# A two-image convolution: three loads move one pair later in the queue, nine fp32 buffers and five bf16 ones in place of eight and six

## The chip, the core and the metric

The kernel runs on one core of a Trainium2 chip. The metric is device microseconds of one execution. Engines are named as in the profile: PE (TensorE, matrix products), DVE (VectorE), ACT (ScalarE), POOL (GpSimd), SP (SyncE, which here only issues transfers). The core has 16 DMA engines, which move data between HBM and on-chip memory.

## The reference

A 3 x 3 convolution with padding 1 over 16 images of 64 channels and 64 x 64 points, to 128 output channels, all in fp32. About 90% of the weights are zero, but the kernel treats them as dense.

```python
x_pad = np.pad(x, ((0, 0), (0, 0), (pad, pad), (pad, pad)), mode='constant')
for b, co, ci, kh, kw in ...:          # all of them, written as nested loops
    output[b, co] += weight[co, ci, kh, kw] * x_pad[b, ci, kh:kh+h, kw:kw+w]
```

Input is 16.8 MB, output 33.6 MB.

## The kernel before, in words

**Pairs.** Two images make a pair: their 64 channels each fill the 128 partitions. There are eight pairs, 0 to 7. `load(p)` brings pair p (2 MB, 16 KiB a partition) into an fp32 buffer of the pool `f`; the queue is SP's. `cast_x` turns it into a bf16 buffer of the pool `x`, in pieces of rows that ACT, POOL and (for pair 0) DVE take. The two results of a pair, one of 2 MB for each image, are written into two more buffers of the same pool `f` and stored from there. So the pool `f` serves loads and results alike, in the order in which the program asks for them: a new one takes a buffer that an older load or result has left, and its first writer waits until the casts have read the old load, or the store of the old result has landed.

**Blocks.** A pair is worked in four blocks of 16 rows. In a block of `twos` (all but the first block of pair 0), POOL adds neighbouring rows into `s` (L161), PE multiplies `s` by the middle row of taps, ACT copies that shared product from PSUM to `pc` (L168), and PE makes two further products, for the even and the odd rows; DVE adds each to `pc` and writes the result buffer (L175). A block is 30 matmuls on PE, one addition on POOL, two copies on ACT and four additions on DVE. `s` has three buffers, so POOL works up to three blocks ahead of PE. [...] `direct` does the same for one block with nine taps a row.

**Casts.** A hand-written table says after which block of which pair a piece is cast. For the inputs 4 to 7 it is filled by a loop: in pair p, after block 1, ACT casts rows 0 to 16 of input p + 2; after block 3 ACT casts rows 16 to 32 and POOL rows 32 to 64.

**The order.** Each engine executes its instructions in the order in which the program writes them (the schedule is manual). SP's queue holds the weights, loads 0 to 4, and then for each pair its two stores and one further load; the last pair is stored in four halves. A transfer that has to wait holds up those behind it on SP. The loop is this:

```python
for p in range(NP):
    o = [f_pool.tile([C_OUT, H, W], FP32, name="f") for _ in range(2)]
    ...                                 # the four blocks and their casts
    if not last:
        for n in range(2):
            nc.sync.dma_start(out=out[2 * p + n], in_=o[n])
    if p + 5 < NP:
        load(p + 5)
```

Below, L5 is load 5, 3A and 3B are the results of pair 3 or their stores, and x4 is the bf16 buffer of pair 4.

Of the kernel before, what the change touches and what calls it, by code (L numbers as in the profile page):

```python
# [27 lines left out]
def kernel(  # L28
# [11 lines left out]
    NP = B // 2  # L40
    HEAD = 32

    const_pool = ctx.enter_context(tc.tile_pool(name="const", bufs=1))
    x_pool = ctx.enter_context(tc.tile_pool(name="x", bufs=6))
    s_pool = ctx.enter_context(tc.tile_pool(name="s", bufs=3))
    p_pool = ctx.enter_context(tc.tile_pool(name="pc", bufs=4))

    f_pool = ctx.enter_context(tc.tile_pool(name="f", bufs=8))
    psum_pool = ctx.enter_context(
        tc.tile_pool(name="psum", bufs=8, space=bass.MemoryType.PSUM)  # L50
    )
# [7 lines left out]
    def load(p, *cuts):  # L59
        src = x[2 * p : 2 * p + 2].rearrange("n i h w -> (n i) h w")  # L60
        raw[p] = f_pool.tile([128, H, W], FP32, name="f")
        for a, b in zip((0, *cuts), (*cuts, H)):
            nc.sync.dma_start(out=raw[p][:, a:b, :], in_=src[:, a:b, :])

    def cast_x(copy, p, a, b):
        if p not in xs:
            xs[p] = x_pool.tile([128, H, W], BF16, name="x")
        copy(out=xs[p][:, a:b, :], in_=raw[p][:, a:b, :])  # L68
# [82 lines left out]
    def direct(p, o, r0, rows):  # L151
        ps = product(
            [(xs[p], G1, r0, 1), (xs[p], G0, r0 - 1, 1), (xs[p], G2, r0 + 1, 1)], rows
        )
        nc.scalar.copy(out=o[0][:, r0 : r0 + rows, :], in_=ps[0])  # L155
        nc.vector.tensor_copy(out=o[1][:, r0 : r0 + rows, :], in_=ps[1])  # L156

    def twos(p, o, r0):
        t0 = r0 // 2
        s = s_pool.tile([128, 8, W], BF16, name="s")  # L160
        nc.gpsimd.tensor_tensor(  # L161
            out=s, in0=xs[p][:, r0 : r0 + 16 : 2, :], in1=xs[p][:, r0 + 1 : r0 + 16 : 2, :], op=ADD
        )
        shared = product([(s, G1, 0, 1)], 8)
        pc = []
        for n in range(2):
            c = p_pool.tile([128, 8, W], FP32, name="pc")
            nc.scalar.copy(out=c, in_=shared[n])  # L168
            pc.append(c)
        even = [(xs[p], G21, r0 + 1, 2), (xs[p], G0, r0 - 1, 2)]  # L170
        odd = [(xs[p], G01, r0, 2), (xs[p], G2, r0 + 2, 2)]
        for first, terms in ((r0, even), (r0 + 1, odd)):
            ps = product(terms, 8)
            for n in range(2):
                nc.vector.tensor_tensor(  # L175
                    out=o[n][:, first : r0 + 16 : 2, :], in0=ps[n], in1=pc[n], op=ADD
                )


    ACT, POOL = nc.scalar.copy, nc.gpsimd.tensor_copy  # L180
    casts = {
        (0, 1): [(POOL, 0, 48, H)],
        (0, 2): [(ACT, 1, 0, 16)],
        (0, 3): [(ACT, 1, 16, 32), (POOL, 1, 32, H)],
        (1, 0): [(ACT, 2, 0, 16)],
        (1, 1): [(ACT, 2, 16, 32), (POOL, 2, 32, H)],
        (1, 2): [(ACT, 3, 0, 16)],
        (1, 3): [(ACT, 3, 16, 32), (POOL, 3, 32, H)],
    }
    for p in range(2, 6):  # L190
        casts[p, 1] = [(ACT, p + 2, 0, 16)]
        casts[p, 3] = [(ACT, p + 2, 16, 32), (POOL, p + 2, 32, H)]

    for p in range(NP):
        o = [f_pool.tile([C_OUT, H, W], FP32, name="f") for _ in range(2)]
        last = p == NP - 1
        for blk in range(4):
            r0 = 16 * blk
            if BLOCKS[p][blk] == "T":
                twos(p, o, r0)  # L200
            else:
                for r, rows in ((r0, 8), (r0 + 8, 8)):
                    direct(p, o, r, rows)
            for cast_of in casts.get((p, blk), ()):
                cast_x(*cast_of)
            if last and blk % 2 == 1:
                for n in range(2):
                    rows = slice(r0 - 16, r0 + 16)
                    nc.sync.dma_start(out=out[2 * p + n][:, rows, :], in_=o[n][:, rows, :])
        if not last:  # L210
            for n in range(2):
                nc.sync.dma_start(out=out[2 * p + n], in_=o[n])
        if p + 5 < NP:
            load(p + 5)


# [28 lines left out]
```

## Time and profile before

| | us |
|---|---|
| median of 5 runs | 128.56 (128.5 to 128.68) |
| the profiled execution | 128.62 |
| its span in the profile | 126.8 |
| PE busy | 109.9 (87%) |
| DVE busy | 82.4 (65%) |
| ACT busy | 52.3 (41%) |
| POOL busy | 50.6 (40%) |
| data queue, share of 16 DMA engines | 95.5% |

The span runs from the first to the last instruction that the profiler saw; the time of an execution has 1.8 us around it. The profile gives busy time for each engine, the span in 40 slices of 3.17 us, and for each idle stretch of an engine the event that ended it (the releaser). A transfer has an issue on SP's timeline and a time to landing; it has landed when all DMA engines that share it are done.

### The profile page before, as it was taken

The page shows a single profiled execution, that of the slowest core. Times are in us where ns is not written, and L with a number is a line of the kernel's source. Part 1 is how long each engine was busy: PE and PEld are TensorE (multiplying, and loading weights), DVE is VectorE, ACT ScalarE, POOL GpSimd, SP SyncE. Part 2 cuts the span into 40 slices and gives each one's busy share as a digit, 9 for nine tenths or more (in the row PEclk, how much of TensorE's full clock was granted, in tenths as well). Part 3 has the DMA queues.
Part 4 walks back from the last instruction along what each step waited for, and adds up shares of the span by engine and source line. Part 5 has one row for each costly group of instructions (what it writes and reads, how often), then busy time and mean ns, then how long its engine had stood idle before and what let it go on. Part 6 is the DMA issues. An engine that isn't in the chain of part 4 may idle for free.

```text
span 126.8 us, 2519 instructions
## 1 busy us (share of the span) xinstructions
PE 109.9 (87%) x1002; PEld 61.0 (48%) x1002; DVE 82.4 (65%) x136; ACT 52.3 (41%) x85; POOL 50.6 (40%) x45
## 2 busy tenths in 40 slices
PE   6589999999999799969999999999999999992000
PEld 6334545567776255534555555555555555550000
DVE  0382577877760999239978778777877777776000
ACT  4542466666636336333636363636333333330000
POOL 2059613998375323913366335733333330000000
PEclk9968999999999999999999999999999999999855
DMA  4999999999999999999999999999999969999990
GB/s 134 413 444 429 434 429 429 419 264 429 439 419 424 429 426 444 419 421 429 434 429 419 434 419 434 429 419 431 424 434 434 413 284 413 419 411 413 424 393 36
DMA packets 4044, 50.79 MB, mean 400 GB/s; under 512 B 448, under 2 KB 448, under 8 KB 576
## 3 DMA queue, kind: packets, MB, share of 16 engines
q1 hardware_dynamic: 4032, 50.63, 95.5%
q8 instruction: 8, 0.13, 0.4%
q14 instruction: 4, 0.03, 0.1%
HBM read 17.07 MB, written 33.55 MB: 399 GB/s over the span
## 4 chain that ended last, share of the span: by engine, by line
PE 65%; DMA 19%; DVE 4%; issue 1%; DVEq 1%; SPq 0%
PE ps L142 65%; DMA out_dram<-f 15%; DMA f<-in_x_dram 4%; DVE f L175 4%; DVEq L240 0%; DVE x L68 0%; SPq L71 0%; DVEq L175 0%
## 5 line engine op out<-in xcount | busy, mean ns | idle before, releaser
L142 PE MATMUL ps<-x,wT 64*128 64x504 bf16 (+3 forms) x780 | 94.9, 378 | 2.2 <-DVE x L68 1.7
L175 DVE TENSOR_TENSOR f<-ps,pc 128x512 f32<-128x512 f32 x124 | 77.1, 685 | 25.9 <-PE ps L142 19.1
L142 PEld LDWEIGHTS <-wT 64*128 64x128 bf16 x966 | 57.8, 95 | 51.9 <-issue 7.5
L161 POOL TENSOR_TENSOR s<-x 128x512 bf16<-128x512 bf16 x31 | 35.6, 1155 | 52.0 <-PE ps L142 40.3
L168 ACT COPY pc<-ps 128x512 f32<-128x512 f32 x62 | 33.4, 589 | 53.7 <-issue 39.7
L142 PE MATMUL ps<-s,wT 64*128 64x512 bf16 (+1 forms) x186 | 30.1, 377 | 1.6 <-DVE f L175 1.6
L68 ACT CAST x<-f 128x1024 bf16<-128x1024 f32 (+2 forms) x16 | 16.3, 1026 | 0.7 <-DMA f<-in_x_dram 0.7
L68 POOL CAST x<-f 128x2048 bf16<-128x2048 f32 (+1 forms) x8 | 14.8, 1845 | 1.0 <-DMA f<-in_x_dram 1.0
L83 PE MATMUL ps<-idle_rhs 128*128 128x128 bf16 x27 | 2.9, 306 | 1.0 <-DVE idle_rhs L80 1.0
L83 PEld LDWEIGHTS <-idle_rhs 128*128 128x128 bf16 x27 | 2.8, 148 | 1.0 <-DVE idle_rhs L80 1.0
L97 DVE CAST w_bf<-w_sb 128x192 bf16<-128x192 f32 (+1 forms) x4 | 1.1, 351 | 2.7 <-DMA w_sb<-in_weight_dram 2.7
L155 ACT COPY f<-ps 128x512 f32<-128x512 f32 x2 | 1.2, 586 | 4.1 <-PE ps L142 4.1
L156 DVE COPY f<-ps 128x512 f32<-128x512 f32 x2 | 1.4, 692 | 2.2 <-PE ps L142 2.2
L68 DVE CAST x<-f 128x576 bf16<-128x576 f32 (+1 forms) x2 | 1.3, 641 | 2.1 <-DMA f<-in_x_dram 2.1
L97 ACT ACT_TABLE_LOAD x1 | 1.3, 1283 | 0.7 <-PEq L229 0.7
L97 ACT CAST w_bf<-w_sb 128x64 bf16<-128x64 f32 (+1 forms) x2 | 0.7, 418 | 1.6 <-DMA w_sb<-in_weight_dram 1.6
L103 PE MATMUL ps<-ident,w_bf 128*128 128x128 bf16 x9 | 0.9, 223 | 0.3 <-DVE w_bf L97 0.3
L107 DVE TENSOR_TENSOR wT<-ps,wT 128x384 bf16<-128x384 f32 x2 | 1.0, 548 | 0.0
L103 PEld LDWEIGHTS <-w_bf 128*128 128x128 bf16 x9 | 0.5, 98 | 0.7 <-DVE w_bf L97 0.7
L80 DVE MEMSET idle_rhs<- 128x64 uint32 x1 | 0.1, 112 | 0.8 <-PEq L229 0.8
L116 ACT CAST wT<-ps 128x384 bf16<-128x384 f32 x1 | 0.5, 479 | 0.2 <-PE ps L103 0.2
L118 DVE CAST wT<-ps 128x384 bf16<-128x384 f32 x1 | 0.6, 551 | 0.0
(7 smaller groups left out, 1.4 us busy)
## 6 DMA issues: line engine op xcount, KB each, us to landing
out_dram<-f SPq DMA_DIRECT2D x14, 2048.0 KB, 15.8
f<-in_x_dram SPq DMA_DIRECT2D x7, 2048.0 KB, 22.1
out_dram<-f SPq DMA_DIRECT2D x4, 1024.0 KB, 9.4
f<-in_x_dram SPq DMA_DIRECT2D x2, 1024.0 KB, 6.1
w_sb<-in_weight_dram SPq DMA_DIRECT2D x1, 288.0 KB, 2.9
```

What stands on the lines that cost most here:

```text
L68: copy(out=xs[p][:, a:b, :], in_=raw[p][:, a:b, :])
L83: nc.tensor.matmul(idle_ps, idle_rhs, idle_rhs, start=True, stop=True)
L97: copy(out=w_bf4[:, g, a:b, :], in_=w_v[:, k : k + b - a, :])
L103: nc.tensor.matmul(wps[:, j, :], src, ident, start=True, stop=True)
L107: nc.vector.tensor_tensor(out=wT[:, g], in0=wps, in1=wT[:, G1], op=SUB)
L118: nc.vector.tensor_copy(out=wT[:, G0], in_=ps0)
L142: nc.tensor.matmul(ps[n][:, lo:hi, c_lo:c_hi], tap(g, kw, n), src[q, a:b:step, c_lo + kw - 1 : c_hi + kw - 1], start=(i == 0), stop=(i == ...
L155: nc.scalar.copy(out=o[0][:, r0 : r0 + rows, :], in_=ps[0])
L156: nc.vector.tensor_copy(out=o[1][:, r0 : r0 + rows, :], in_=ps[1])
L161: nc.gpsimd.tensor_tensor(out=s, in0=xs[p][:, r0 : r0 + 16 : 2, :], in1=xs[p][:, r0 + 1 : r0 + 16 : 2, :], op=ADD)
L168: nc.scalar.copy(out=c, in_=shared[n])
L175: nc.vector.tensor_tensor(out=o[n][:, first : r0 + 16 : 2, :], in0=ps[n], in1=pc[n], op=ADD)
```

## The change

Three edits. The pool `x` has five buffers in place of six, the pool `f` nine in place of eight. The loads 5, 6 and 7 stand behind the stores of the pairs 1, 2 and 3 in SP's queue, where they stood behind those of the pairs 0, 1 and 2. ACT's first piece of the casts of inputs 4 to 7 stands after block 2 of its pair in place of block 1.

```diff
-    x_pool = ctx.enter_context(tc.tile_pool(name="x", bufs=6))
+    x_pool = ctx.enter_context(tc.tile_pool(name="x", bufs=5))
...
-    f_pool = ctx.enter_context(tc.tile_pool(name="f", bufs=8))
+    f_pool = ctx.enter_context(tc.tile_pool(name="f", bufs=9))
...
     for p in range(2, 6):
-        casts[p, 1] = [(ACT, p + 2, 0, 16)]
+        casts[p, 2] = [(ACT, p + 2, 0, 16)]
         casts[p, 3] = [(ACT, p + 2, 16, 32), (POOL, p + 2, 32, H)]
...
-        if p + 5 < NP:
-            load(p + 5)
+        if 5 <= p + 4 < NP:
+            load(p + 4)
```

## The prediction, made before the changed kernel was run

> **What bounds the kernel now.** I read the slices of the page first, for which resource is full all along; then the DMA queues; then stretches of the tail; last the timelines of the engines around the holes.
>
> The slices and the queue rows of the page (each digit is a fortieth of the span in tenths; a queue row gives packets, MB and share of 16 engines' span):
> ```profile
> PE   6589999999999799969999999999999999992000
> DMA  4999999999999999999999999999999969999990
> q1 hardware_dynamic: 4032, 50.63, 95.5%
> q8 instruction: 8, 0.13, 0.4%
> ```
> Both rows are full nearly throughout, but PE stops at slice 37 and DMA doesn't. 50.63 MB at the 427 to 430 GB/s of the middle stretches take 118 us of a span of 126.8: the transfers are the bound, and PE is close behind. PE has two holes, near slices 13 and 17; DMA has one, slice 32.
>
> The stretches around slice 32 and the end (us, PE clock, DMA share of 16 engines, GB/s):
> ```profile
> 98.00:101.00 3.00, 1.00 1.02 437
> ...
> 102.00:103.00 1.00, 1.00 0.39 164
> 103.00:104.00 1.00, 1.00 0.70 295
> 104.00:107.00 3.00, 1.00 1.01 426
> ...
> 122.00:124.00 2.00, 0.50 0.78 324
> 124.00:126.00 2.00, 0.50 0.10 41
> ```
> At 102 most DMA engines have run dry. They start again about 1.2 us after the next stores are issued at 102.84. But not all ran dry: store 5B (pair 5, second image) was issued at 90.64 and took 15.0 us to land whole, so some engine worked on it until 105.6. The last row says the same of the end: a share of 0.10 is 1.6 engines of 16. **The end is set by one or two late DMA engines that had no hole.** From 105.6 they land 6A at 110.7, 6B at 115.9, and the last store at 116.25 + 9.5 = 125.75. That is 20.15 us for 8.4 MB, where four spacings of the steady stretch (4.87 us for 2 MB) make 19.5. At most 0.65 us is to be had there.
>
> The holes of PE, in the DVE timeline (start, us, instruction, idle before and its releaser):
> ```profile
> 37.00 0.69 DVE L175 TENSOR_TENSOR f<-ps,pc 128x512 f32<-128x512 f32 x1 [0.69 <-POOL s L161]
> 41.37 7.27 DVE L175 TENSOR_TENSOR f<-ps,pc 128x512 f32<-128x512 f32 x12 [3.68 <-PE ps L142]
> ...
> 55.97 9.06 DVE L175 TENSOR_TENSOR f<-ps,pc 128x512 f32<-128x512 f32 x15 [4.16 <-DMA out_dram<-f]
> ```
> DVE waits twice for an output buffer whose store is under way: until 41.37 for that of store 0B (23.52 + 17.7 = 41.2; the label names PE, which was long done), until 55.97 for that of 1B (36.33 + 19.5 = 55.8). PSUM fills and PE waits in turn. Pairs start on PE (first product of s) at 34.77, 48.87, 63.46, 76.27, 89.07, 101.88 for pairs 2 to 7: pair 2 takes 14.1, pair 3 14.6, the rest 12.8. The stalls cost PE 3.1 us.
>
> [...] The trace agrees (0.39 of the engines busy at 102, whole landing at 105.6); so below every landing is that of the last engine. [...] The q8 row, 0.13 MB in 8 packets, fits that; I suppose, without a row for each engine, that these packets make some engines late. The change leaves PE's instructions as they are, so I keep the lateness.
>
> **The change part by part.** No instruction is added or removed. PE, DVE and POOL keep their order, SP moves three loads behind two stores each, ACT moves four casts by one block.
>
> *Stalls removed.* As built, the first writes of pair 2 wait for load 1's buffer and store 0A (landed 36.4, written from 37.7), those of pair 3 for 0B (41.2, against about 50) and a cast buffer. Both stalls go: pair 3 starts at 34.77 + 12.81 = 47.6, pair 4 at 60.4. The gain is 3.1 us of PE.
>
> *Loads later.* The queue is first in, first out and full, so places in it are times. From the issue and landing of each transfer before, the places after load 4 (31.5) land whole at 36.4, 41.2, 46.0, 51.0, 55.8, 61.3, 66.3, 71.1, 75.9, 80.9, 85.7. Before they are 0A 0B L5 1A 1B L6 2A 2B L7 3A 3B; after, 0A 0B 1A 1B L5 2A 2B L6 3A 3B L7. SP has issued each before its place comes (1A at 35.7; 2A by about 48.8; 3A by 61.6), so no gap opens. Behind a moved load on SP stand only the next pair's stores, which wait for DVE longer still; each takes SP 0.3 to 1.2 us to issue. L5 lands at 55.8, L6 at 71.1, L7 at 85.7, each 9.8 later, while pairs come sooner.
>
> *Who waits for a load.* POOL casts half of it, and its timeline in pair 4 shows how early:
> ```profile
> 64.61 1.16 POOL L161 TENSOR_TENSOR s<-x 128x512 bf16<-128x512 bf16 x1 [2.00 <-PE ps L142]
> 65.71 1.89 POOL L68 CAST x<-f 128x2048 bf16<-128x2048 f32 x1
> 67.80 1.15 POOL L161 TENSOR_TENSOR s<-x 128x512 bf16<-128x512 bf16 x1 [0.20 <-PE ps L142]
> ```
> The cast stands 2.25 us after the pair's start; behind it is the sum s for the next pair's first block, which PE needs 12.8 after the start. From landing to that product: 1.89 cast, 1.15 sum, 0.2 of hand-overs, 3.25 us. A landing later than 9.55 us after the pair's start stalls PE one for one. ACT's limit is nearly the same: the copy of the last block stands at +10.5 (73.99 in pair 4) and the cast ahead of it takes 1.06, so landing after +9.45 delays it and DVE behind it, by at most the PE stall itself; DVE has 0.6 to 0.7 us of idle time a block to catch up. I count no more for ACT.
> Pair 3: L5 at +8.2, no stall, POOL idles instead. Pair 4: L6 at 71.1 - 60.4 = +10.7, stall 1.15; pair 5 starts at 74.35. Pair 6 can start at 85.7 + 3.25 = 88.95 (stall 1.8). Before it was 89.07. **The 3.1 us are given back as waits for loads**, and the sum at pair 6 is -0.1.
>
> *The tail.* Pair 7 starts 0.1 earlier, 6A is issued at about 102.7, the early engines run dry as before, the late ones don't notice. Gain 0 to 0.3; I take 0.1. In pair 2 ACT's cast of x4 moves too: its load landed at 31.5 and its first reader, POOL, comes at about 52, so it costs nothing. Five bf16 buffers cost nothing: pair 5's takes that of pair 0, last read around 22. Both pools take 9 x 16 + 5 x 8 = 184 KiB a partition in place of 176.
>
> Sum: profiled 128.62 (span 126.8 and 1.8 around it) less 0.1; the median of the runs is 0.06 lower, and with half of the possible 0.3 in place of 0.1 I say **128.4**.
>
> **The rivals.**
> *Loads come in time (faster).* The share falls from 101 on; less the 1.2 us of start, 6A issued by about 100, nearly 3 us sooner than worked out, leaves no engine dry, and if what the late engines lose after 102 comes of all starting together, they save up to the 0.65: about 127.95. That needs L7 by 83. For it: the places carry 2 to 3 us of lateness of single engines, which may differ. Against: the loads' places follow from bytes alone.
> *Waits for loads overtake the slack (slower).* The late engines are free at 105.6; less 1.2 us of start, 6A may be issued up to 104.4, 1.6 later than before. That is L7 landing later than 87.4. From there each microsecond adds one: at 88.3, 129.4. It needs 2 to 3% less transfer rate before 86. For it: four stores now follow each other at 31 to 51, and PE twice waits on a load with nothing buffered. Against: stretches with loads mixed in (427 to 429) and of stores alone (427) have one rate.
> *The change doesn't do what it says.* The order as built shows the moved loads and the new waits, so I give this nothing.
> *The gain goes through whole (faster).* The 3.1 us show up in the end: 125.5. The full queue speaks against it; under 1 in 20.
>
> **How the numbers follow.** A measurement here tells about 0.2% (0.26 us) from no change. Stalls exchanged, tail as it was: 0.60, giving 128.1 to 128.85, mostly within the bound (0.48 same, 0.09 faster, 0.03 slower). Loads in time or gain whole: 0.23 (0.21 faster, 0.02 same). Slack overtaken: 0.17, all slower. Sum: faster 0.30, same 0.50, slower 0.20. The range 127.9 to 129.2 reaches into both outer cases; the likeliest case alone is 128.1 to 128.85.
>
> **What would show it.** DVE's two waits for stores gone, pair 3 at 47.6 and pair 4 at 60.4; POOL casts waiting for f loads at about 49.8 to 55.8, 62.6 to 71.1 and 76.6 to 85.7; PE stalled for s before pairs 5 and 6; pair 6 within half a microsecond of 89; slice 32 of DMA still low; the last landing near 125.6. Pair 6 before 88 or after 90.6, or a DMA row without a hole, would prove the working wrong.

## The result, and the profile after

Medians: 128.54 us for the changed kernel (43 runs), 128.65 for the kernel before (80 runs). The ratio is 0.9992, 95% interval 0.9981 to 1.0004: no difference that the measurement can tell. The prediction was 128.4 with "same" the likeliest. The profiled execution of the changed kernel took 129.26 us, so it stands 0.7 above its median and its span of 127.5 is compared with care.

The slices and the data queue in the page of the changed kernel:
```profile
PE   6689999999999999999999989996899999991000
DMA  4999999999999999999999999999999989999990
q1 hardware_dynamic: 4032, 50.63, 95.9%
```
PE's holes near slices 13 and 17 are gone. Two others have come, near slices 23 and 27. The DMA row is full as before, and its one weak slice is still slice 32.

DVE's timeline in pairs 2 and 3 of the changed kernel (start, us, instruction, idle before and its releaser):
```profile
38.26 2.48 DVE L175 TENSOR_TENSOR f<-ps,pc 128x512 f32<-128x512 f32 x4 [0.69 <-POOL s L161]
41.41 2.51 DVE L175 TENSOR_TENSOR f<-ps,pc 128x512 f32<-128x512 f32 x4 [0.67 <-PE ps L142]
...
50.96 2.53 DVE L175 TENSOR_TENSOR f<-ps,pc 128x512 f32<-128x512 f32 x4 [0.58 <-ACT pc L168]
```
No wait for a store is left; every gap is the usual 0.6 to 0.7 us. (In the profile before, PE waited four times for DVE's L175, 2.1 us in total; in this one it doesn't. The kernel's PSUM pool has eight buffers and a block takes six, so DVE's waits soon left PE nowhere to write.)

POOL's timeline of the changed kernel, the casts of loads 5, 6 and 7 with the sums behind them:
```profile
49.86 1.15 POOL L161 TENSOR_TENSOR s<-x 128x512 bf16<-128x512 bf16 x1 [2.01 <-PE ps L142]
57.38 1.89 POOL L68 CAST x<-f 128x2048 bf16<-128x2048 f32 x1 [6.37 <-PE ps L142]
59.23 4.58 POOL L161 TENSOR_TENSOR s<-x 128x512 bf16<-128x512 bf16 x4
72.02 1.89 POOL L68 CAST x<-f 128x2048 bf16<-128x2048 f32 x1 [8.20 <-DMA f<-in_x_dram]
73.87 4.50 POOL L161 TENSOR_TENSOR s<-x 128x512 bf16<-128x512 bf16 x4
86.53 1.89 POOL L68 CAST x<-f 128x2048 bf16<-128x2048 f32 x1 [8.16 <-DMA f<-in_x_dram]
```
The new waits are here, 6.4, 8.2 and 8.2 us. The first is labelled PE, but it ends with the landing of load 5 (issued 38.02, 19.3 us to landing). POOL then catches up with several sums in a row. Only at the second and third cast is it too late for PE, as PE's timeline shows, where pairs 5 and 6 begin:
```profile
75.08 0.82 PE L142 MATMUL ps<-s,wT 64*128 64x512 bf16 x6 [0.40 <-POOL s L161]
...
89.58 0.83 PE L142 MATMUL ps<-s,wT 64*128 64x512 bf16 x6 [1.52 <-POOL s L161]
```
The pairs 2 to 7 start at 36.03, 48.84, 61.64, 75.08, 89.58 and 102.39. So pairs 2 and 3 take 12.8 us each, pair 4 takes 13.4 and pair 5 takes 14.5: 2.3 us of stalls in place of 3.1.

The tail of the changed kernel by stretches (us, PE clock, DMA share, GB/s):
```profile
101.00:102.00 1.00, 1.00 1.13 475
102.00:103.00 1.00, 1.00 0.91 377
103.00:104.00 1.00, 1.00 0.47 197
...
124.00:126.00 2.00, 0.50 0.19 78
```
The hole comes about a microsecond later than before (0.39 in the stretch from 102, 0.70 in the next). The share of so short a stretch is rough: it counts a packet where it starts, so that it can pass 1 (1.13 above), and a data packet of 16 KiB took 0.61 us here (the median of 2696). The trace also keeps 16 landings of each transfer, one for each DMA engine, without the engine's name; they are exact, and are used below. The first engine is done with 5B at 103.32 instead of 101.80, the last at 106.36 instead of 105.64, and 6A, the first store of pair 6, is issued at 103.35 instead of 102.84. At the end again only a few engines work: 12 of 16 have done the last store at 124.7, the last one at 126.4.

### The profile page after: what moved, and what is told of

Read it like the earlier page. It is cut to its first block, busy times and chain, and to the rows that moved or that the text cites. A ratio compares the mean times of both kernels' runs of the same rounds, so it can differ in the third digit from the quotient of the medians.

```text
span 127.5 us, 2520 instructions
## 1 busy us (share of the span) xinstructions
PE 110.9 (87%) x1002; PEld 66.1 (52%) x1002; DVE 83.0 (65%) x136; ACT 52.3 (41%) x85; POOL 50.3 (39%) x45
## 4 chain that ended last, share of the span: by engine, by line
PE 59%; issue 18%; POOL 7%; DMA 4%; DVE 1%; DVEq 0%; SPq 0%; POOLq 0%
PE ps L142 59%; POOL s L161 7%; DMA f<-in_x_dram 4%; DVE f L175 1%; DVEq L240 0%; DVE x L68 0%; SPq L71 0%; POOL x L68 0%; POOLq L161 0%; DVEq L175 0%
## 5 line engine op out<-in xcount | busy, mean ns | idle before, releaser
L175 DVE TENSOR_TENSOR f<-ps,pc 128x512 f32<-128x512 f32 x124 | 77.7, 685 | 24.5 <-PE ps L142 17.0
L142 PE MATMUL ps<-x,wT 64*128 64x504 bf16 (+3 forms) x780 | 92.2, 382 | 1.4 <-DVE x L68 1.4
L142 PEld LDWEIGHTS <-wT 64*128 64x128 bf16 x966 | 62.5, 96 | 47.2 <-issue 7.4
L142 PE MATMUL ps<-s,wT 64*128 64x512 bf16 (+1 forms) x186 | 26.1, 377 | 1.9 <-POOL s L161 1.9
L116 ACT CAST wT<-ps 128x384 bf16<-128x384 f32 x1 | 0.5, 479 | 0.4 <-PE ps L103 0.4
L120 ACT CAST wT<-ps 128x384 bf16<-128x384 f32 x1 | 0.5, 479 | 0.2 <-PE ps L103 0.2
```

The lines of the kernel that those rows point to most:

```text
L116: nc.scalar.copy(out=wT[:, G1], in_=transposed(G1))
L142: nc.tensor.matmul(ps[n][:, lo:hi, c_lo:c_hi], tap(g, kw, n), src[q, a:b:step, c_lo + kw - 1 : c_hi + kw - 1], start=(i == 0), stop=(i == ...
L175: nc.vector.tensor_tensor(out=o[n][:, first : r0 + 16 : 2, :], in0=ps[n], in1=pc[n], op=ADD)
```

## The experiments

Each run is compared with the kernel before, run on the same chip beside it. "Span" is that of the run's profiled execution.

**The buffers alone.** Edit to the kernel before:
```diff
-    x_pool = ctx.enter_context(tc.tile_pool(name="x", bufs=6))
+    x_pool = ctx.enter_context(tc.tile_pool(name="x", bufs=5))
-    f_pool = ctx.enter_context(tc.tile_pool(name="f", bufs=8))
+    f_pool = ctx.enter_context(tc.tile_pool(name="f", bufs=9))
```


> The buffer part alone: nine fp32 and five bf16 buffers, loads and casts where they stood before. Pair 3's results then wait for 1A at most (51.0, written from about 50.5) instead of 1A and 1B, pair 2's for 0A (36.4). So neither the waits for stores nor those for loads are left: pair 3 should start on PE near 47.6, pair 7 near 98.8 instead of 101.9, and 6A be issued at about 99.8, before any DMA engine runs dry; slice 32 of DMA full. Theory (the end is set by the late DMA engines, which never had a hole): the end moves by 0 to -0.65 us only, 128.0 to 128.65. Rival (PE's 3.1 us of stalls were on the path, and the change lost them again to waits for loads): 125.5.


Measured: ratio 0.9981 (0.9966 to 0.9996), 128.2 us; span 126.8. PE's row and the tail of this run:
```profile
PE   6649999999999999999999999999999999990000
...
101.00:102.00 1.00, 1.00 0.76 311
102.00:103.00 1.00, 1.00 0.85 360
103.00:104.00 1.00, 1.00 1.02 426
```
No stall is left on PE after slice 3; every pair takes 12.8 us. The DMA hole is nearly closed. The gain is 0.2%, not the 2.4% that 3.1 us would be: the first theory holds on this side. In this execution 6A was issued at 101.83, not 99.8 as expected, because PE's first product of `s` came 2.1 us later than before (14.38 instead of 12.32): its first block of pair 0 was slow (see the last section).

**The loads alone.** The changed kernel with eight and six buffers again:
```diff
-    x_pool = ctx.enter_context(tc.tile_pool(name="x", bufs=5))
+    x_pool = ctx.enter_context(tc.tile_pool(name="x", bufs=6))
-    f_pool = ctx.enter_context(tc.tile_pool(name="f", bufs=9))
+    f_pool = ctx.enter_context(tc.tile_pool(name="f", bufs=8))
```


> The other part alone: loads and casts moved as in the change, eight fp32 and six bf16 buffers as before. As built, pair 2 then waits for 0A and pair 3 for 1A, whose place in the queue is 46.0, so the waits for stores go without the ninth buffer; the waits for loads are those of the changed kernel. Theory: as the changed kernel in pair starts (within 0.5 us) and in time, 128.3 to 128.8. Rival (the ninth buffer is what removes the waits for stores): both kinds of waits, pair 7 about 3 us later, 129.5 or more.


Measured: 1.0014 (0.9996 to 1.0032), 128.76 us; span 126.6. PE stalls for loads alone:
```profile
74.09 0.82 PE L142 MATMUL ps<-s,wT 64*128 64x512 bf16 x6 [2.20 <-POOL s L161]
...
88.62 0.82 PE L142 MATMUL ps<-s,wT 64*128 64x512 bf16 x6 [1.55 <-POOL s L161]
```
DVE still waits 1.5 us for a store, until 36.24, but PE doesn't stall for it. So each part of the change by itself keeps PE from stalling for stores, and the moved loads alone bring the stalls for loads. Together the two parts cure the same trouble twice, and the cost of the second stays. One more thing is seen: PE was 2.8 us quicker through pair 0 here than in the changed kernel's profile (first s product at 10.79 against 13.58), yet pair 6 starts only 1.0 us earlier. The landing of load 7 holds it (85.5 here, 86.5 there).

**Load 7 one place further back.** Edit to the changed kernel:
```diff
             for n in range(2):
                 nc.sync.dma_start(out=out[2 * p + n], in_=o[n])
-        if 5 <= p + 4 < NP:
+                if p == 4 and n == 0:
+                    load(7)
+        if 5 <= p + 4 < 7:
             load(p + 4)
```


> The changed kernel with load 7 one place further back in the queue, between 4A and 4B: a test of the slack. L7 should land 4.9 later, near 91.3 by the trace after; pair 6 starts at landing + 3.2 = 94.5, pair 7 at 107.3, 6A issued at 108.3, all DMA engines dry before that. Theory (a slack of 1.6 us at the late engines, then one for one): 4.9 - 1.6 = +3.3, up to +4.0, so 132 to 132.6. Rival (the chain through PE ends last, as the chain of waits says): +4.9, 133.5. Rival (transfers alone count): no change, 128.6.


Measured: 1.0559 (1.0523 to 1.0595), 135.74 us; span 134.3. That is 7.2 us, outside all three expectations. Load 7 landed at 76.04 + 15.9 = 91.9, and pair 6 started 3.1 later, as worked out. PE's timeline there, then its clock by stretches (us, PE busy, PE clock, DMA share, GB/s):
```profile
95.03 1.47 PE L142 MATMUL ps<-s,wT 64*128 64x512 bf16 x6 [6.90 <-POOL s L161]
96.27 3.63 PE L142 MATMUL ps<-x,wT 64*128 64x512 bf16 x24
99.72 0.82 PE L142 MATMUL ps<-s,wT 64*128 64x512 bf16 x6
```
```profile
92.00:95.00 3.00, 0.00 (x0) 0.50 0.63 270
95.00:97.00 2.00, 1.97 (x10) 0.50 0.54 229
97.00:99.00 2.00, 2.00 (x16) 0.71 1.05 442
99.00:101.00 2.00, 2.00 (x22) 1.00 0.92 393
```
After 6.9 us without work PE was granted half its clock, and the first block took 4.7 us instead of 3.2. Pair 7 and 6A came 7.0 later than in the changed kernel's profile (6A at 110.33), and the span is 6.8 longer. The loss passed whole; of a slack of 1.6 us nothing is seen. That called for a test of the slack by itself.

**A slip of pair 6, small and large.** Edit to the kernel before (22 in place of 7 for the large one); the product's first matmul overwrites what the idle ones write:
```diff
-    def product(terms, rows):
+    def product(terms, rows, idle=0):
...
+        for _ in range(idle):
+            nc.tensor.matmul(
+                ps[0], idle_rhs[0:64, :], terms[0][0][0:64, 0:8, :], start=True, stop=True
+            )
...
-        shared = product([(s, G1, 0, 1)], 8)
+        shared = product([(s, G1, 0, 1)], 8, 7 if (p, r0) == (6, 0) else 0)
```


> The kernel before with seven idle matmuls of 512 columns ahead of pair 6's first product, which its first matmul overwrites: pairs 6 and 7 start about 0.8 to 1.5 us later, as read from PE's timeline. Theory (late DMA engines have a slack of 1.6 us there): no change, within 0.3 us. Rival (the chain through PE and the last stores sets the end): later by the slip, 0.8 to 1.5 us.

> The same with 22 idle matmuls: pairs 6 and 7 start about 2.4 to 4.7 us later. Theory: the slip less 1.6 us. Rival (PE chain): the whole slip. Rival (transfers alone): nothing.


Measured: small 1.009 (1.0067 to 1.0114), span 128.3; large 1.0342 (1.0321 to 1.0364), span 131.6. The slips are read from SP's timeline, where 6A is issued: before, with the small slip and with the large one.
```profile
102.84 0.93 SPq L212 DMA_DIRECT2D out_dram<-f  x2
```
```profile
104.33 0.93 SPq L216 DMA_DIRECT2D out_dram<-f  x2
```
```profile
107.64 0.93 SPq L216 DMA_DIRECT2D out_dram<-f  x2
```
The slips are 1.49 and 4.80 us; the spans of the profiles grew by 1.5 and 4.8, the medians of the times by 1.25 and 4.47 (from 128.71 to 129.96 and 133.18). **There is no slack of 1.6 us**, at most one of 0.3. The spans of six profiles follow one rule: 6A's issue plus 24.0 to 24.2 (before 102.84 and 126.8; small slip 104.33 and 128.3; large slip 107.64 and 131.6; load 7 late 110.33 and 134.3; changed 103.35 and 127.5; loads alone 102.39 and 126.6). Call that the ramp. But with 6A at 101.83 the span of the kernel with nine buffers is still 126.8. So there is a floor too, a time below which the end doesn't come however early 6A is. The kernel before stands about where floor and ramp meet: over all runs its median span is 126.8, that with nine buffers 126.4.

How the last store lands shows the two. Its 16 landings, counted from 6A's issue: with the small slip 14 engines at 21.0 to 21.4, one at 21.9, one at 22.9; with the large slip the same. Before, 12 at 21.0 to 21.3, two at 21.8 and 21.9, two at 22.9. So before, a second pair of late engines ends together with the pair that the slips have too. The end of the small slip (us, PE clock, DMA share, GB/s; 0.06 is one engine of 16):
```profile
124.40:125.00 0.60, 0.50 0.88 369
125.00:125.40 0.40, 0.50 0.11 41
125.40:125.90 0.50, 0.50 0.08 33
125.90:126.90 1.00, 0.50 0.06 25
```

**PE's work taken out, its instructions kept.** Edit to the kernel before; of each product only the first matmul covers all rows:
```diff
+            if i > 0:
+                hi = lo + 1
             c_lo, c_hi = max(0, 1 - kw), min(W, W + 1 - kw)
```


> The kernel before with nearly all of PE's work taken out and its instructions kept: of each product only the first matmul covers all rows, the others one row, so the result is not the convolution. PE then runs far ahead of everything, the stores are issued early and the queue is full to the end. Theory: nothing but transfers left, and they were the bound: -0.2 to -0.65, 128.0 to 128.45. Rival (PE and the transfers share the bound through the hole at 102): -2 us or more, 126.5 or less.


Measured: 0.9967 (0.9954 to 0.9979), 128.08 us; span 126.4. The PE row falls to 70.5 us of work, the last store is issued at 104.14, 12 us earlier than before, and the DMA row has no hole:
```profile
DMA  4999999999999999999999999999999999999960
```
It buys 0.4 us. This is the floor: transfers alone, with nothing to wait for. Even so the 16 engines end apart: the last store lands from 121.4 to 125.3.

**Fewer and more PE instructions.** Both on the kernel before: three matmuls for each half of a product and the rest left out; and the light variant with one-row matmuls issued twice. The edits are
```diff
-        todo = [(t, kw) for t in terms for kw in KW_ORDER]
+        todo = [(t, kw) for t in terms for kw in KW_ORDER][:3]
```
```diff
+            if i > 0:
+                hi = lo + 1
...
-            for n in range(2):
+            for n in (0, 1) if i == 0 or i == len(todo) - 1 else (0, 1, 0, 1):
```


> The kernel before with three matmuls for each half of every product (those of its first term) and the rest left out, so the result is not the convolution: PE's instructions fall from 2006 to 1214 and its time with them, while the transfers are the same. To be compared with the run with light PE work (126.4 span, last landing 125.33, first engine done at 121.41), which keeps all instructions. Theory that instruction fetches through the DMA engines make the late engines late: 4 or 5 fetches in place of 8, so the latest engine is 1 to 2.5 us earlier, 125.6 to 127.1. Rival (lateness comes of the data transfers themselves): as light PE, 128.0 to 128.3.

> The light-PE variant of the kernel before, with every matmul of one row that is not the last of its product issued twice, so the result is not the convolution: about 3200 instructions on PE instead of 2006, some 12 or 13 fetches of instructions instead of 8, at light work and the same transfers. Theory that fetches set the lateness: the latest engine 0.5 to 2 us later than with light PE, 128.6 to 130. Rival (fetches don't matter): 128.0 to 128.3.


Measured: fewer 0.9935 (0.9918 to 0.9953), 127.98 us; more 1.0091 (1.0075 to 1.0107), 130.09 us. The instruction rows of the two pages, fewer first (packets, MB, share):
```profile
q8 instruction: 4, 0.07, 0.2%
```
```profile
q8 instruction: 12, 0.20, 0.6%
```
With 12 packets instead of 8 and the same data, the time rises over light PE by 2.0 us by the medians (130.09 against 128.08) and by 1.6 us by the ratios, though PE is idle at the end of both. That is what the fetch theory expected, in the upper half of its range. With 4 packets it falls by 0.1 us by the medians, 0.4 us by the ratios, where 1 to 2.5 us were expected.

The landings of the last store say why the two differ. With 4, 8 and 12 packets the first engine is done at 121.4, 121.4 and 121.2, the last at 125.0, 125.3 and 127.2, and the mean of all 16 is 122.46, 122.82 and 123.35. The mean moves with the packets both times: as an estimate from these means, each packet costs one engine 1.4 us ((122.82 - 122.46) x 16 / 4) to 2.1 us ((123.35 - 122.82) x 16 / 4). The kernel's time, though, goes with the last engine: the three medians are 2.8 to 3.0 us above its landing. So in these runs more instruction packets go with later landings; that the packets themselves hold engines up is the author's estimate, since no trace says which engine a packet ran on. With 4 of them, 3.6 us still lie between the first and the last, and where that comes from stays open.

**Nine buffers and the small slip.** The two edits above together.

> Nine fp32 buffers with the loads where they stood, and the seven idle matmuls ahead of pair 6 that cost the kernel before 0.9%. Revised theory (the last landing is the later of a floor near 125.5 and 6A's issue plus 23.0): with the stalls gone 6A is issued at 101.8 or earlier, plus 1.5 for the idle matmuls, so at most 103.3: the time is that of the kernel before, within 0.4%, not 0.9% above it. Rival (a slip always counts whole): 1.2 to 1.5 us over the run with nine buffers alone, so 0.7% to 0.9% above before.


Measured: 0.9973 (0.9956 to 0.999), 128.27 us; span 126.5. The seven idle matmuls that cost the kernel before 0.9% cost nothing here. 6A is issued at 99.67 and the rule of 24.0 would give a span of 123.7; the floor decides.

**Nine buffers and 14 idle matmuls.** Edit to the kernel before, with the two buffer counts:
```diff
     nc.scalar.copy(out=wT[:, G2], in_=ps2)
+    for _ in range(14):
+        nc.tensor.matmul(idle_ps, idle_rhs, idle_rhs, start=True, stop=True)
```


> Nine fp32 buffers, loads where they stood, and 14 idle matmuls between the weight transposes and the first product, so that PE doesn't idle ahead of pair 0 (whose first block took 4.0 to 6.9 us in the traces). Revised theory: PE may gain up to 3 us at the start and 6A be issued near 99 to 100, and the time stays at the floor, as with nine buffers alone: -0.1% to -0.4% to before. Rival (PE's time still counts): -1% or more.


Measured: 0.996 (0.9942 to 0.9977), 128.12 us; span 126.4. Its first block on PE, 6A on SP, and the DMA row:
```profile
6.93 3.99 PE L144 MATMUL ps<-x,wT 64*128 64x512 bf16 x36 [0.95 <-DVE x L68]
```
```profile
98.19 1.39 SPq L214 DMA_DIRECT2D out_dram<-f  x2
```
```profile
DMA  4999999999999999999999999999999999999960
```
6A is issued 4.6 us earlier than before and the gain is 0.4%, that of the light PE. It is the fastest kernel here that computes the whole convolution, ahead of both (its interval ends at 0.9977, the changed kernel's begins at 0.9981), and it stands on the floor. From the two other runs with nine buffers (0.9966 to 0.9996 and 0.9956 to 0.999) it can't be told apart. That the 14 idle matmuls brought 6A forward isn't shown either: the run with the small slip and nine buffers has none of them, its first block took 3.99 us too, and its 6A less the slip of 1.5 us comes at 98.2 as well. Nine buffers don't take all of DVE's waits for stores away when PE is that early; these two, for 0A and 1A, are left, and PE doesn't stall for them:
```profile
36.37 4.88 DVE L177 TENSOR_TENSOR f<-ps,pc 128x512 f32<-128x512 f32 x8 [1.64 <-DMA out_dram<-f]
...
50.97 6.67 DVE L177 TENSOR_TENSOR f<-ps,pc 128x512 f32<-128x512 f32 x11 [2.06 <-DMA out_dram<-f]
```

## Why the prediction was right, and where it was not

*Stalls removed*: right. DVE's two waits for stores are gone and pairs 2 and 3 take 12.8 us. The absolute starts, 48.84 and 61.64, are 1.2 later than 47.6 and 60.4, since PE took 6.88 us for pair 0's first block in this execution, 5.67 in the one before.

*Loads later*: right. Loads 5, 6 and 7 landed at 57.3, 71.9 and 86.5 where 55.8, 71.1 and 85.7 were worked out; the order of places held, and the lateness was 0.8 to 1.5 us. Load 5's 1.5 us come mostly of one slice near 52 us, in which the page has 283 GB/s where the slices around it have 386 and more; what slowed the transfers there is open.

*Who waits for a load*: right. Pair 6 starts 3.1 us after the landing (3.25 worked out), pair 5's stall before it is 1.7 (1.8), that of pair 4 is 0.6 (1.15 worked out; most of the difference is that pair 4 began 1.2 later than worked out and load 6 landed only 0.9 later). Pair 6 starts at 89.58 instead of 88.95. The loads-only run shows that this part of the change brings these waits, and the buffers-only run shows that the other part doesn't.

*The tail*: the sum came out, one step under it failed. "The late ones don't notice" and the limit of 104.4 for 6A in the slower rival took the engines that end last for those that were late at 105.6, and put any lateness that comes up after 6A at nothing. The slips show that the span follows 6A one for one from 102.84 on. In both slips 6A lands whole 6.4 us after its issue, in place of 7.9 before, where the first engine had done with it after 6.1 (108.96 less 102.84). That leaves 0.3 of lateness, so in the slips all DMA engines start nearly together. Yet the end is as far from 6A's issue as before, so lateness of that size is made again in the tail. The slack was at most 0.3 us, not 1.6.

What makes it was not tried by itself, but the landings fit an instruction packet of 16 KiB, of which the tail has one in each slip (0.9 and 1.0 us long; the eight of the profile before took 0.88 to 1.05). In the small slip it runs from 11.7 to 12.6 us after 6A's issue; the latest landing of 6B, at 12.2, is 1.0 late, that of the next store 2.0 late. In the large slip it runs from 10.1 to 11.1, and the latest landing of 6B is 2.0 late already. The 2.0 us are within the 1.4 to 2.1 estimated above. Which engine the packet ran on isn't recorded, and the engine that ends 0.9 late isn't explained; one instruction packet of 8 KiB, 9.2 us after 6A's issue in both slips, is all else that the tail moves beside the stores.

So the result was "same" because 6A hardly moved, since the waits for loads replaced those for stores within half a microsecond, and not because a slack took up the rest. That the false limit did no harm was luck: by the rule of 24.0, had the change delayed 6A by 1 us more, the kernel would have been slower by about 0.8%, and the prediction would have missed it.

Three readings under that step were rough. "At 102 most DMA engines have run dry" rests on the share of 0.39; by the landings two of 16 were done with 5B at 102, seven at 103, 13 at 104 and the last at 105.64. And "a share of 0.10 is 1.6 engines" at the end is four late engines, landing at 124.7, 124.7, 125.7 and 125.8. The third, "about 1.2 us after" the issue, is 0.8 to 1.0 for the first packets (before, in stretches of 0.1 us):
```profile
103.50:103.60 0.10, 1.00 0.38 164
103.60:103.70 0.10, 1.00 1.92 819
103.70:103.80 0.10, 1.00 2.69 1147
```
Counted to the landing 1.2 holds: 6.1 to 6A's first, less 4.9 for 2 MB.

*What could be gained*, 0 to 0.65 us: right; light PE, which has nothing else to win, gained 0.4 us, nine buffers with the 14 idle matmuls 0.5.

*The rivals*: "loads come in time" is what the buffers alone do, and that gains 0.2 to 0.4% in the three runs that have them. "The gain goes through whole" (125.5) is refuted by the same run and by light PE.

## What to carry to other kernels

Here the transfers were the bound, and 3.1 us of stalls removed from PE gained 0.2 to 0.4%: they could count only through 6A, the one transfer before which the queue ran dry, and only down to the floor. In a kernel like it, find that transfer's issue, and ask what sets it. Before counting on slack at the end, ask which of two ends is meant, that of the engines that never paused or that of those that restart. Here the two lay together: 6A 4.6 us earlier gained 0.4%, 1.49 us later lost 1.25 us. A buffer and a reordering that cure the same wait are tried one by one: here one was a small gain, the other brought a wait of its own.

## What the runs showed of the hardware that was not expected

PE's first block of pair 0, the same 36 matmuls, took 3.99 us with the loads alone, 5.67 before, 6.57 with the buffers alone and 6.88 in the changed kernel. With 14 idle matmuls just ahead of it the profiled execution took 3.99, as two executions without them did (loads alone, small slip), so the idle matmuls aren't shown to help. The granted clock in the profile didn't tell the slow start each time: from 7 to 11 us it reads 0.52 and 0.63 before and 1.00 in the changed kernel, while PE works on 14 and 14 matmuls and on 12 and 14 (two stretches of 2 us each); the quick block of the small slip has 21 and 22.

After two of three later idle stretches the granted clock was lower. After 6.9 us without work (load 7 late) the granted clock read 0.50 until 97 us and 0.71 on average until 99, and the first block took 4.7 us instead of 3.2. After 2.1 us (small slip, at 42 us) it fell to 0.50 from 44 to 46, and 23 matmuls took 4.34 us that took 2.75 before; after 2.2 us (loads alone, at 74 us) it stayed at 1.00. Why the one stretch cost clock and the other, as long, did not is open.

The eight instruction packets (q8) of the profile before, 16 KiB each, took 0.95 us in the median, data packets of the same size 0.61. The run with twelve of them (0.20 MB), which also has more PE instructions, was 1.6 to 2.0 us longer than the run with light PE, which has eight.
